# One decoder block: the first weight half goes to the head of SyncE's DMA queue, the norm weights to GpSimd's

## The chip, the core and the metric

The program runs on one core of a Trainium2 chip. The metric is the device time of one execution in microseconds, as the median of several runs; lower is better. The engines are named as in the profile: PE is TensorE's matmul side, PEld its weight load, DVE is VectorE, ACT is ScalarE, POOL is GpSimd, and SP is SyncE, which here only issues DMAs. A "q" behind an engine's name (SPq, ACTq, POOLq) is its queue of instructions that are not counted as busy, DMA issues among them.

## The reference

One layer of a decoder block in fp32, for 512 tokens (S) of width 1024 (D). The part that this change touches is the very beginning:

```python
h = rmsnorm(x, norm_attn_g)
u = h @ w_in                      # q | k | v | u_pool | u_gate
# then: differential attention on q, k, v; a causal pooling of u_pool; sigmoid gates;
x = x + (sigmoid(g_A) * A + sigmoid(g_P) * P) @ w_out
x = x + relu(rmsnorm(x) @ w_up)**2 @ w_down
return rmsnorm(x)
```

## The kernel before

All products are made of three fp32r matmuls: each operand is split into a high part (`hi`, rounded to fp32r) and a low part (`lo`, the rest), and `hi*hi + lo*hi + hi*lo` is summed in PSUM.

The first stage computes V, the values. x arrives transposed, as 8 tiles of 128 x 512 (`xT[k]`, k = 0 to 7), and lands in the tile `gx` (`gt0` in the code). V's weight `w_v` comes in pieces of 128 x 1024 (`wr_v`), each holding the weight rows of two values of k, and each piece is fetched in two halves of 128 x 512, one for each k. In the profile the tile names carry what they hold: `wr_` a raw weight, `wh_` and `wl_` its high and low part, `xh`, `xla` and `xlb` the high and low parts of x times the norm weight (xla for k = 0 to 3, xlb for 4 to 7), `con` the small constants whose first 8 columns are the norm weights `g1c`, `onesr` a 128 x 128 tile of ones.

For each k this has to happen before PE can do its 12 matmuls (three for each of the four token tiles t):

- x's tile lands (L182 issues it on SP's queue; for k = 0 two halves, L143, on ACT's queue);
- ACT multiplies by the norm weight and rounds: `xh` (L184); DVE makes the rest: `xla` or `xlb` (L185). For k = 0 both are done in halves of 256 columns, so that two of the four token tiles can start early. These need `g1c`;
- the weight half lands (L106, L224), ACT casts it (L112, `wh_v`), DVE subtracts (L113, `wl_v`).

PE's three matmuls are L235 (xh by wh), L236 (xh by wl) and L237 (xl by wh). Beside this ACT squares x (L193, L196) and POOL sums the squares into `ssx` (L197). PE also gets matmuls of the first q head as soon as its weight (`wr_q`, split on ACT and DVE as well) is there: L212, L213 and L214, three for each k. All this is issued through a scheduler that orders each engine's instructions from its own model of their times, so a change at the start of the program can reorder instructions further on. Ahead of all this PE is kept busy by 8 matmuls of ones by ones (L170, 16 in the profile), which need nothing but `onesr`.

Of the kernel before, what the change touches and what calls it, by code (L numbers as in the profile page):

```python
# [12 lines left out]
F32R = mybir.dt.float32r  # L13
# [5 lines left out]
P = 128  # L19
# [32 lines left out]
def block_kernel(ctx, tc, xT, x_tok, gains, pos, consts, w_in, w_v, w_pool, w_out, w_up, w_dn, out):  # L52
    nc = tc.nc
    V, A, G, T = nc.vector, nc.scalar, nc.gpsimd, nc.tensor
# [10 lines left out]
    cp = ctx.enter_context(tc.tile_pool(name="cp", bufs=1))  # L65
# [21 lines left out]
    def tmp(tag, name, shape=(P, S), dt=F32, bufs=2):  # L87
        return tp.tile(list(shape), dt, tag=tag, name=name, bufs=bufs)

    def f(ap):  # L90
        return ap.bitcast(F32)
# [4 lines left out]
    def load_w(src, name, nsplit=1, parts=None):  # L96

        nraw[0] += 1
        third = nraw[0] % 3 == 0 and ctx1_open
        raw = (tp if third else wp).tile([P, 1024], F32, tag="wr3" if third else "wr", name=f"wr_{name}", bufs=1 if third else 2)  # L100
        if nsplit == 1:
            nc.sync.dma_start(out=raw, in_=src)
        else:
            w = 1024 // nsplit
            for i in range(nsplit)[parts or slice(None)]:
                nc.sync.dma_start(out=raw[:, i * w : (i + 1) * w], in_=src[:, i * w : (i + 1) * w])  # L106
        hi = wp.tile([P, 1024], F32R, tag="wh", name=f"wh_{name}", bufs=4)
        lo = wp.tile([P, 1024], F32R, tag="wl", name=f"wl_{name}", bufs=4)
        return raw, hi, lo
# [29 lines left out]
    g1c, g2c, gfc, pscc = (con[:, 8 * i : 8 * i + 8] for i in range(4))  # L139

    gt0 = tmp("g", "gx0", (P, 4, S), bufs=1)
    for i in range(2):
        nc.scalar.dma_start(out=gt0[:, 0, i * 256 : i * 256 + 256], in_=xT[0, :, i * 256 : i * 256 + 256])  # L143
    A.preload_act_table_set(EXPLN)
    nc.sync.dma_start(out=g1c, in_=consts[:, 0:8])
    wv0 = load_w(w_v[0, 0], "v0_0", 2, slice(0, 1))
    invc = con[:, 32:40]
    rcc = con[:, 40:56]
    subc = con[:, 56:57]
# [4 lines left out]

    ident = cp.tile([P, P], F32, name="ident")
    make_identity(nc, ident)
    onesr = cp.tile([P, P], F32R, name="onesr")
    ones = f(onesr)
    G.memset(ones, 1.0)
    eps = cp.tile([P, 1], F32, name="eps")  # L160
    G.memset(eps, EPS)
    mask = cf.tile([P, S], F32, name="mask")
# [2 lines left out]
        out=mask[:, 384:512], in_=mask[:, 384:512], pattern=[[-1, P]],  # L165
# [51 lines left out]
    for n in range(2):  # L217
        accs = [bank((0, 1, 2, 3, 4, 5, 6, 0)[4 * n + t], f"v{n}_{t}") for t in range(NT)]
        for kk in range(4):
# [24 lines left out]
            if n == 0 and 0 < kk < 3:  # L244
                i = kk - 1
# [14 lines left out]
        for t in range(NT):  # L260
# [4 lines left out]
                out=vd[2], in0=av, scalar=rcol[:, t, 0:1], in1=vd[1],  # L265
# [26 lines left out]
        out=r_, in0=posf.rearrange("p (t o) -> p t o", o=1).to_broadcast(sh),  # L292
# [700 lines left out]
```

## Time and profile before

| | |
|---|---|
| three runs | 676.32, 676.32, 677.84 us |
| median | 676.32 us |
| profiled execution: span from first to last instruction | 675.2 us |
| PE busy | 665.3 us, 99% of the span |
| DVE, ACT, POOL busy | 529.1, 462.5, 123.0 us |
| first matmul of V (L235) starts | 5.11 us |
| PE's one wait behind the start of V's first pass ends (L237) | 22.20 us |

The profile gives no other time of the profiled execution than its span; the runs' median stands 1.1 us above it. Times in the text are microseconds from the span's start. In a row of the timeline the first number is the start, the second the time, "x2" says that two instructions are merged into the row, and what stands in brackets is how long the engine had been idle before and what ended that. In a row of waits the numbers are the sum, the count and the longest. In a list of DMA issues the last number is the time from issue to landing.

### The profile page before, as it was taken

To read this page: it belongs to the slowest core of one execution; us is meant where nothing else is said; L and a number is where in the kernel's file an instruction comes from. 1 tells how busy PE (TensorE), PEld (TensorE's weight loads), DVE (VectorE), ACT (ScalarE), POOL (GpSimd) and SP (SyncE) were. 2 spreads that over 40 slices of the span, in tenths; PEclk is the share of its full clock that TensorE was granted. 3 is DMA by queue.
4 is the path that set the end of the run, shared out by engine and by line. 5 is a ranking of instruction groups with operands and counts; after the bars stand their busy time and mean duration, and the time that the engine had idled before them with its cause. 6 is when DMAs were issued, how large, how long until landed. Compare 5 with 4: busy or idle time off the path is not lost.

```text
span 675.2 us, 9995 instructions
## 1 busy us (share of the span) xinstructions
PE 665.3 (99%) x3686; PEld 579.9 (86%) x3686; DVE 529.1 (78%) x879; ACT 462.5 (68%) x741; POOL 123.0 (18%) x137
## 2 busy tenths in 40 slices
PE   9999999999999999999999999999999999999995
PEld 7788888888888888888889988899889998899884
DVE  6955877799979986975478989667994599747995
ACT  8465587978887698883477975367753696356874
POOL 6201110132133212520201020202103021210120
PEclk9999999999999999999999999999999999999999
DMA  8526574435254364574964678676969579493863
GB/s 272 189 71 182 126 152 125 102 94 126 87 139 105 101 171 94 126 193 177 309 194 79 196 172 241 153 179 155 234 190 197 200 156 260 125 213 131 213 125 124
DMA packets 32880, 109.34 MB, mean 162 GB/s; under 512 B 4032, under 2 KB 4928, under 8 KB 32832
## 3 DMA queue, kind: packets, MB, share of 16 engines
q0 software_dynamic: 10656, 38.80, 32.4%
q1 hardware_dynamic: 21744, 69.38, 29.0%
q8 instruction: 29, 0.48, 0.3%
q10 hardware_dynamic: 432, 0.52, 0.2%
q14 instruction: 19, 0.16, 0.1%
HBM read 106.59 MB, written 2.10 MB: 161 GB/s over the span
## 4 chain that ended last, share of the span: by engine, by line
PE 86%; DMA 5%; issue 5%; DVE 1%; ACT 1%; SPq 0%; DVEq 0%; POOLq 0%
PE dm L838 7%; PE dm L840 7%; PE dm L841 7%; PE um L759 7%; PE um L764 7%; PE um L761 7%; DMA wga_uNone<-w_up 5%; PE o L417 2%; PE ga L132 2%; PE ga L131 2%; PE gp L135 2%; PE k L132 2%; PE gp L132 2%; PE gp L131 2%; PE k L131 2%
## 5 line engine op out<-in xcount | busy, mean ns | idle before, releaser
L840 PE MATMUL dm<-wh_dt,z 128*128 128x512 f32 (+1 forms) x128 | 49.5, 387 | 0.0
L841 PE MATMUL dm<-wl_dt,z 128*128 128x512 f32 (+1 forms) x128 | 49.4, 386 | 0.0
L838 PE MATMUL dm<-wh_dt,z 128*128 128x512 f32 (+1 forms) x128 | 49.0, 387 | 0.0
L759 PE MATMUL um<-gss,wh_ut 128*128 128x256 f32 x192 | 48.1, 284 | 0.1
L761 PE MATMUL um<-gss,wh_ut 128*128 128x256 f32 x192 | 48.1, 283 | 0.0
L400 ACT ACTIVATE p<-p,st 128x128 f32<-128x128 f32 (+3 forms) x64 | 35.8, 560 | 14.1 <-DVE st L396 13.8
L112 ACT CAST wh_ut<-wga_uNone 128x1024 fp32r<-128x1024 f32 x24 | 24.9, 1053 | 28.8 <-PE dm L840 19.2
L856 DVE TENSOR_TENSOR x<-x,dm 128x512 f32<-128x512 f32 x48 | 32.8, 687 | 14.1 <-PE dm L841 14.0
L670 POOL DMA_DIRECT2D wga_dNone<-w_dn x16 | 14.2, 887 | 151.8 <-DVE wl_dt L113 151.8
L113 DVE TENSOR_TENSOR wl_ut<-wga_uNone,wh_ut 128x1024 fp32r<-128x1024 f32 x24 | 29.0, 1224 | 12.5 <-ACT wh_ut L112 12.5
L112 ACT CAST wh_ub<-wr_u 128x1024 fp32r<-128x1024 f32 x24 | 25.1, 1051 | 19.0 <-PE um L761 10.1
L670 POOL DMA_DIRECT2D wga_uNone<-w_up x18 | 15.6, 867 | 120.9 <-DVE wl_ut L113 86.9
L840 PE MATMUL dm<-wh_db,z 128*128 128x512 f32 x96 | 37.2, 389 | 0.0
L841 PE MATMUL dm<-wl_db,z 128*128 128x512 f32 x96 | 37.2, 389 | 0.0
L759 PEld LDWEIGHTS um<-gss,wh_ut 128*128 128x128 f32 x192 | 36.8, 192 | 0.3 <-ACT rawz L776 0.3
L761 PEld LDWEIGHTS um<-gss,wh_ut 128*128 128x128 f32 x192 | 36.9, 192 | 0.0
L838 PE MATMUL dm<-wh_db,z 128*128 128x512 f32 x96 | 35.8, 390 | 0.0
L113 DVE TENSOR_TENSOR wl_ub<-wr_u,wh_ub 128x1024 fp32r<-128x1024 f32 x24 | 29.2, 1222 | 7.9 <-ACT wh_ub L112 7.9
L112 ACT CAST wh_dt<-wga_dNone 128x1024 fp32r<-128x1024 f32 x24 | 24.8, 1050 | 14.6 <-issue 4.1
L735 DVE TENSOR_TENSOR z<-rawz,z 128x1024 fp32r<-128x1024 f32 x28 | 33.7, 1225 | 0.9 <-ACT z L732 0.9
L396 DVE CUSTOM_DVE_ANT_0 p<-s,mask 128x128 f32<-128x128 f32 (+3 forms) x64 | 30.3, 485 | 3.4 <-PE s L395 3.3
L732 ACT CAST z<-rawz 128x1024 fp32r<-128x1024 f32 x28 | 28.7, 1048 | 6.0 <-DVE rawz L741 4.9
(324 smaller groups left out, 2222.9 us busy)
## 6 DMA issues: line engine op xcount, KB each, us to landing
wr_u<-w_up SPq DMA_DIRECT2D x24, 512.0 KB, 5.3
wr_d<-w_dn SPq DMA_DIRECT2D x24, 512.0 KB, 4.2
wga_uNone<-w_up POOLq DMA_DIRECT2D x18, 512.0 KB, 6.7
wga_dNone<-w_dn POOLq DMA_DIRECT2D x16, 512.0 KB, 5.8
wr_k<-w_in SPq DMA_DIRECT2D x8, 512.0 KB, 3.3
wr_ga<-w_in SPq DMA_DIRECT2D x8, 512.0 KB, 3.3
wr_gp<-w_in SPq DMA_DIRECT2D x8, 512.0 KB, 4.2
wl_ga<-w_in POOLq DMA_DIRECT2D x8, 512.0 KB, 5.5
```

Of the source, the lines that this page charges most:

```text
L112: ins = A.copy(out=hi[:, sl], in_=raw[:, sl])
L113: (eng or G).tensor_tensor(out=lo[:, sl], in0=raw[:, sl], in1=f(hi)[:, sl], op=ALU.subtract)
L131: T.matmul(acc, lhsT=hi[:, c], rhs=rh[:, k, :], start=k == 0, stop=False)
L132: T.matmul(acc, lhsT=hi[:, c], rhs=rl[k], start=False, stop=False)
L400: A.activation(out=pr[:, c, :N], in_=pr[:, c, :N], func=AF.Exp, scale=-1.0, bias=st[:, c : c + 1], accum_out=st[:, 2 + c : 3 + c])
L735: V.tensor_tensor(out=z[:, 1], in0=r, in1=f(z[:, 0]), op=ALU.subtract)
L759: m = T.matmul(a_, lhsT=hi[:, c], rhs=rh[:, k, :], start=p + k == 0 and onto is None, stop=False, skip_group_check=True)
L761: T.matmul(a_, lhsT=hi[:, c], rhs=rl[:, k, :], start=False, stop=False, skip_group_check=True)
L764: m = T.matmul(a_, lhsT=lo[:, c], rhs=rh[:, k, :], start=False, stop=k == 3, skip_group_check=True)
L838: m = T.matmul(a_, lhsT=zh, rhs=hi[:, sl], start=p == 0 and start, stop=False, skip_group_check=True)
L840: T.matmul(a_, lhsT=zl, rhs=hi[:, sl], start=False, stop=False, skip_group_check=True)
L841: end = T.matmul(a_, lhsT=zh, rhs=lo[:, sl], start=False, stop=p == 3, skip_group_check=True)
```

## The change

Four edits, all ahead of the loops:

- `onesr` is set by VectorE (`V.memset`) as its first instruction, and no longer by GpSimd behind the identity's memset;
- the first half of V's first weight is the first DMA on SP's queue, where `g1c` stood;
- `g1c` is fetched by GpSimd's queue, as POOL's first instruction;
- the second half of x's first tile moves from ACT's queue to SP's, behind that weight half.

```diff
     gt0 = tmp("g", "gx0", (P, 4, S), bufs=1)
-    for i in range(2):
-        nc.scalar.dma_start(out=gt0[:, 0, i * 256 : i * 256 + 256], in_=xT[0, :, i * 256 : i * 256 + 256])
+    onesr = cp.tile([P, P], F32R, name="onesr")
+    ones = f(onesr)
+    V.memset(ones, 1.0)
+    nc.scalar.dma_start(out=gt0[:, 0, 0:256], in_=xT[0, :, 0:256])
+    wv0 = load_w(w_v[0, 0], "v0_0", 2, slice(0, 1))
+    G.dma_start(out=g1c, in_=consts[:, 0:8])
     A.preload_act_table_set(EXPLN)
-    nc.sync.dma_start(out=g1c, in_=consts[:, 0:8])
-    wv0 = load_w(w_v[0, 0], "v0_0", 2, slice(0, 1))
+    nc.sync.dma_start(out=gt0[:, 0, 256:512], in_=xT[0, :, 256:512])
...
-    onesr = cp.tile([P, P], F32R, name="onesr")
-    ones = f(onesr)
-    G.memset(ones, 1.0)
```

What this does to the engines' orders shows at three places. The numbers in the names only tell tiles apart (`wr_v0_0` is V's first weight piece, `wr_v0_1` the second; `gx0` is x's tile). First SP's queue at the program's start, before:

```order
L145 DMA con_73<-consts 128x8
L106 DMA wr_v0_0_79<-w_v 128x512
L224 DMA wr_v0_0_79<-w_v 128x512
L182 DMA gx0_74<-xT 128x512 x2
L106 DMA wr_v0_1_163<-w_v 128x512 x2
```

and now:

```order
L106 DMA wr_v0_0_78<-w_v 128x512
L149 DMA gx0_74<-xT 128x256
L224 DMA wr_v0_0_78<-w_v 128x512
L182 DMA gx0_74<-xT 128x512 x2
L106 DMA wr_v0_1_163<-w_v 128x512 x2
```

The weight half is one place earlier, x's second half stands in the place that it left, and everything from L224 on keeps its place.

Second, ACT at the program's start, before:

```order
L143 DMA gx0_74<-xT 128x256 x2
L144 ACT_TABLE_LOAD
L184 ACTIVATE xh_84<-gx0_74,con_73 128x256
L112 CAST wh_v0_0_81<-wr_v0_0_79 128x512
L184 ACTIVATE xh_84<-gx0_74,con_73 128x256
L193 ACTIVATE ssx_110<-gx0_74 128x512
L112 CAST wh_v0_0_81<-wr_v0_0_79 128x512
L184 ACTIVATE xh_84<-gx0_74,con_73 128x512
```

and now:

```order
L145 DMA gx0_74<-xT 128x256
L148 ACT_TABLE_LOAD
L112 CAST wh_v0_0_80<-wr_v0_0_78 128x512
L184 ACTIVATE xh_86<-gx0_74,con_73 128x256 x2
L193 ACTIVATE ssx_110<-gx0_74 128x512
L112 CAST wh_v0_0_80<-wr_v0_0_78 128x512
L184 ACTIVATE xh_86<-gx0_74,con_73 128x512
```

ACT now casts the weight half ahead of both halves of x's first tile.

Third, PE ahead of and in the matmuls for k = 4 (weight piece `v0_2`), and behind those for k = 6 (weight piece `v0_3`), as a difference:

```order
 L213 MATMUL q_115<-xla,wh_q_208 128x512
 L214 MATMUL q_115<-xh,wl_q_209 128x512
-L212 MATMUL q_115<-xh,wh_q_208 128x512
 L235 MATMUL v_0_116<-wh_v_2_218,xh 128x512
 L235 MATMUL v_1_117<-wh_v_2_218,xh 128x512
 L235 MATMUL v_2_118<-wh_v_2_218,xh 128x512
 L235 MATMUL v_3_119<-wh_v_2_218,xh 128x512
-L213 MATMUL q_115<-xla,wh_q_208 128x512
 L236 MATMUL v_0_116<-wl_v_2_219,xh 128x512
```

```order
 L236 MATMUL v_3_119<-wl_v_3_272,xh 128x512
 L237 MATMUL v_3_119<-wh_v_3_271,xlb 128x512
+L212 MATMUL q_115<-xh,wh_q_208 128x512
+L213 MATMUL q_115<-xla,wh_q_208 128x512
 L214 MATMUL q_115<-xh,wl_q_209 128x512
 L235 MATMUL v_0_116<-wh_v_3_271,xh 128x512
```

Two matmuls of the q head have moved from the stretch ahead of k = 5 to behind k = 6. Beside these, PE's first 12 matmuls are in another order (two L236 follow the first two L235 at once), DVE's list begins with the memset and the weight's subtraction, ACT does one square (L196 of k = 6) ahead of a cast instead of behind it, and POOL makes the identity's second step (masks.py:199) later. From V's second pass on the orders are the same.

## The prediction

> **What bounds the kernel now.** I read the page's busy times first, then PE's waits over the whole span, then the chain of work that ended last, and then the first 23 us engine by engine.
>
> ```profile
> PE 665.3 (99%) x3686; PEld 579.9 (86%) x3686; DVE 529.1 (78%) x879; ACT 462.5 (68%) x741; POOL 123.0 (18%) x137
> ...
> PE h2T L629 <- ACT h2f L646: 0.6, 1, 0.6
> PE v L237 <- DVE con L282: 0.3, 1, 0.3
> PE v L235 <- ACT wh_v L112: 0.2, 1, 0.2
> ```
>
> PE is busy for 665.3 of 675.2 us, so at most 10 us can be won without taking matmuls away. The change touches the start, where PE waits twice: 0.2 us for the first cast weight and 0.3 us at an L237. The chain of work says what the second hangs on:
>
> ```profile
> 2.12 4.71 DMA gx<-xT
> ...
> 6.85 0.73 ACT xh L184
> ...
> 20.37 1.77 DVE xlb L185
> 22.15 0.07 DVE con L282
> 22.22 0.48 PE v L237
> ```
>
> The chain goes through SP's fourth DMA (x's tile 1, issued at 2.12, landed at 6.83), then ACT, then DVE up to 22.15 and only there reaches PE. So V's start at 5.11 is not on the path: whatever PE wins at the head it must give back at that L237 unless DVE's low part of x (xlb for k = 5) is ready earlier too. This is the point on which the forecast turns.
>
> **The first weight half.** ACT at the start, and the DMAs that it waits for:
>
> ```profile
> 1.67 1.28 ACT L144 ACT_TABLE_LOAD   x1 [1.67 <-PEq L983]
> 4.44 0.62 ACT L112 CAST wh_v<-wr_v 128x512 fp32r<-128x512 f32 x1 [0.83 <-DMA wr_v<-w_v]
> 4.96 0.51 ACT L184 ACTIVATE xh<-gx,con 128x256 fp32r<-128x256 f32 x1
> 5.37 0.62 ACT L193 ACTIVATE ssx<-gx 128x512 f32<-128x512 f32 x1
> 5.94 0.62 ACT L112 CAST wh_v<-wr_v 128x512 fp32r<-128x512 f32 x1
> 6.85 0.73 ACT L184 ACTIVATE xh<-gx,con 128x512 fp32r<-128x512 f32 x1 [0.29 <-DMA gx<-xT]
> ...
> 0.74 0.38 SPq L145 DMA_DIRECT2D con<-consts  x1
> 1.18 0.42 SPq L106 DMA_DIRECT2D wr_v<-w_v  x1
> ...
> gx<-xT ACTq DMA_DIRECT2D x1, 128.0 KB, 2.3
> wr_v<-w_v SPq DMA_DIRECT2D x1, 256.0 KB, 3.2
> con<-consts SPq DMA_DIRECT2D x1, 4.0 KB, 2.0
> ```
>
> The cast waited 0.83 us for the weight, which was issued at 1.18 and took 3.2 us. At the queue's head it is issued at 0.74. Its time to landing is bounded from below by x's half, 2.3 us for half the bytes, and from above by its own 3.2; I take the middle, 2.75, since it now shares the engines with one half of x instead of two. It lands at 3.5 (3.05 to 3.95). The table load has ended by then (one DMA issue less on ACT's queue, 0.45 us by the distance of two issues on SP; nobody waits for it). The cast then runs from 3.5 to 4.1, and ACT's next instruction starts 0.52 us after it (4.44 to 4.96), at 4.02.
>
> **The norm weights by POOL.** They are now needed at 4.02, before at 3.1. No such small DMA on POOL's queue is in the trace; the nearest rows are POOL's first big one and the small one on SP's queue, each with the stretch in which its first packets appear:
>
> ```profile
> wl_u<-w_in POOLq DMA_DIRECT2D x1, 512.0 KB, 5.6
> q0 software_dynamic: 11, 0.05, 264.0%
> DMA packets 6, 0.00 MB, mean 0 GB/s; under 512 B 6, under 2 KB 6, under 8 KB 6
> L122 POOL DMA_DIRECT2D wl_u<-w_in x1: 999/999/999, 60.5 to 60.5; - x1
> ```
>
> POOL's DMA, issued at 60.5, has no packet on its queue q0 in the stretch 60.4 to 62.2 and its first 11 in 62.2 to 62.4 (second line): 1.7 us. On SP's queue the first 6 packets of the program fall before 1.75 (third line), 1.0 us after the issue at 0.74. So POOL costs 0.7 us more: 2.0 + 0.7 = 2.7 us to landing as the lower bound, and 5.6 us, with 128 times the bytes, as the upper. The small row is far nearer in size; with 0.3 us for standing beside 384 KB of weight and x, I take 3.0: landed at 3.75, hidden behind the cast by 0.3 us. At the upper bound it lands at 6.35. ACT's order past that point (0.41 each for the two halves of xh, 0.57 for the square, 0.62 for the second cast, by the distances of starts above) leaves xh for k = 1 at its old 6.85 if the first half starts by 4.85, so that is how late the constants may be without any cost to the chain.
>
> The Trainium skill, DMA: Bandwidth & Descriptors, Specifications, gives about 1 us to the first byte for GpSimd's path and 0.6 for SyncE's; the trace has 1.7 and 1.0, so the measurement decides. By the page's 0.4 us the constants would land at 3.45 and the sum be the same.
>
> On POOL the issue (1.0 us, last line above) stands ahead of the memsets, where `onesr`'s 0.2 us goes away, so POOL's preparation ends 0.8 us later. The next thing on POOL, the first sum of squares at 8.18, comes after 2.25 us of idling (its row is below). That is the cover; 1.4 us of it is left.
>
> **The warm-up matmuls, and PE's start.**
>
> ```profile
> 0.88 0.20 POOL L159 MEMSET onesr<- 128x128 f32 x1
> ...
> 1.14 0.58 PE L170 MATMUL warm<-onesr 128*128 128x128 f32 x1 [1.14 <-POOL onesr L159]
> 4.07 0.85 PE L170 MATMUL warm<-onesr 128*128 128x128 f32 x3
> 5.11 1.22 PE L235 MATMUL v<-wh_v,xh 128*128 128x512 f32 x2 [0.19 <-ACT wh_v L112]
> 6.13 0.78 PE L235 MATMUL v<-wh_v,xh 128*128 128x512 f32 x2
> 6.75 0.40 PE L236 MATMUL v<-wl_v,xh 128*128 128x512 f32 x1
> ```
>
> DVE has nothing before 3.6, so its memset can start with the program, at about 0.70, and take about POOL's 0.20: PE starts at 0.95 instead of 1.14, and the warm-up's last matmul ends at 4.73 instead of 4.92 (4.07 + 0.85). The first xh half ends at 4.02 + 0.51 = 4.53, so V starts at 4.6, as the next matmul's start overlaps the last one's end (by about 0.2: 0.40 us each, 0.23 apart, below). These first matmuls run slowly: 1.02 us for the first two (5.11 to 6.13), 0.62 for the next two, of which the second already has the later pace of 0.23, so about 0.4 for a slow one. By 6.5 half a microsecond of earlier start has bought only one matmul (starts at 4.6, 5.1, 5.6, 6.0 and 6.4 against 5.1, 5.6, 6.1 and 6.5): PE's lead at k = 1 is 0.23 to 0.33; I take 0.28. The subtraction that L236 needs, DVE's first real work, ends at 4.1 + 0.69 and is wanted at 5.6.
>
> **The two moved matmuls, and the sum.** Further on:
>
> ```profile
> 17.43 0.39 PE L212 MATMUL q<-xh,wh_q 128*128 128x512 f32 x1
> 18.34 1.07 PE L235 MATMUL v<-wh_v,xh 128*128 128x512 f32 x4
> 21.51 0.39 PE L236 MATMUL v<-wl_v,xh 128*128 128x512 f32 x1
> 22.20 0.50 PE L237 MATMUL v<-wh_v,xlb 128*128 128x512 f32 x1 [0.30 <-DVE con L282]
> ...
> 8.74 1.32 DVE L185 SCALAR_TENSOR_TENSOR xla<-gx,con,xh 128x512 fp32r<-128x512 f32 x1 [0.39 <-ACT xh L184]
> 13.40 0.74 DVE L185 SCALAR_TENSOR_TENSOR xla<-gx,con,xh 128x512 fp32r<-128x512 f32 x1
> 20.37 1.77 DVE L185 SCALAR_TENSOR_TENSOR xlb<-gx,con,xh 128x512 fp32r<-128x512 f32 x1
> ...
> 8.18 1.33 POOL L197 TENSOR_TENSOR ssx<-ssx,sq 128x512 f32<-128x512 f32 x1 [2.25 <-ACT sq L196]
> 18.61 2.99 POOL L197 TENSOR_TENSOR ssx<-ssx,sq 128x512 f32<-128x512 f32 x2 [1.01 <-ACT sq L196]
> ...
> GB/s 0 0 0 13 212 332 324 279 283 254 258 303 328 385 393 373 381 414 402 406 406 389 397 389 385 377 184 8 0 160 328 365 213 322 287 269 246 319 244 294
> ```
>
> PE's pace is 0.227 us a matmul (four from 17.43 to 18.34). In the old order it would reach that L237 at 21.74 and waits until 22.20, 0.46 us by starts. In the new one L212 and L213 are no longer ahead of it: PE is there at 21.74 - 0.28 - 0.45 = 21.0. But xlb for k = 5 comes when DVE has made it, and the two matmuls are still to be done afterwards: **+0.45 us** behind the wait.
>
> DVE's end is the other term. From 8.74 to 22.14 DVE does not pause, and its order there is unchanged. One such operation takes 0.74 us where no sum of squares runs on POOL and 1.77 where one does; seven sums fall into this stretch, from 8.18 to 21.6. The chain starts with x's tile 1, which stays fourth on SP's queue with the same 768 KB of x and weight ahead of it. It can gain only from DMA engines idle at the start: of the 40 slices of the first 20 us (last line) the fifth has 212 GB/s and the sixth 332, which is 60 KB or 0.18 us. So the chain moves by 0 to -0.18; I take -0.1.
>
> Sum: -0.1 + 0.45 = **+0.35 us**: 675.2 becomes 675.55, and with the 1.1 us between span and median 676.32 becomes 676.7. That is no change: 0.3%, 2.0 us, is about what a measurement can tell here, and three runs of before spread over 1.5 us. PE's wait at the L237 should grow to about 1.1 us, and the start of V, half a microsecond earlier, be lost in it.
>
> **The rivals.** *DVE's chain gets shorter (faster).* ACT now makes the square for k = 6 ahead of a cast, so the sums shift against DVE's work; if one falls behind xlb for k = 5, the chain is 1.03 us shorter (1.77 - 0.74). Then DVE ends at 21.1, PE is there at 21.0: -1.1 + 0.45 = -0.7, 675.6. For it: the sums lie as close as 18.61 and 20.1 to the chain's end. Against: the shift makes them earlier, and the squares set them before the end in either order.
>
> PE's pace before 6.5 bears on this price. The Trainium skill, TensorE: Matmul & The Clock Gate, Part 1, says that the clock opens after one busy window of 3.4 us that does not start with the program; the trace, with the switch 5.3 us after the first warm-up matmul, agrees. By that rule the switch could as well come 6.8 us after it, at 7.75: PE's lead would be -0.3 instead of 0.28 and this rival 676.2; the forecast stays as it is, since PE would still wait for DVE.
>
> *The constants come late (slower).* Each microsecond beyond 4.85 is one on ACT's xh for k = 1 and so on DVE's chain. At 5.5 the sum is +0.45 + 0.65 = +1.1, 677.4; at the upper bound, 6.35, +1.95, 678.3. It decides against the kernel (over 2.0 us) from a landing at 6.4 on, 5.7 us after the issue. For it: the only POOL row has 5.6 us. Against: that one moves 512 KB, its first packets come after 1.7 us.
>
> [...]
>
> *The change does nothing for the weight:* it shares the DMA engines with x and lands at 3.95 or later. V starts at 5.1; PE still waits for DVE, and the sum is +0.45, 676.8.
>
> **How the numbers follow.** Forecast 0.60, the weight no earlier 0.14 (the same time within a measurement's reach), DVE's chain shorter 0.12, constants late 0.14, of which 0.04 beyond the bound. With 0.02 on each side for a median drawn by the runs' spread: faster 0.03, same 0.91, slower 0.06. The range goes from the shorter chain, less 0.1 (675.5), to the constants at 5.5 plus 0.5 of the runs' spread (677.9). The likeliest case alone is 676.3 to 677.2.
>
> **What would show it.** V's first L235 at 4.5 to 4.7; its cast at 3.5 with no later wait for `con`; the warm-up from 0.95; L212 and L213 for k = 2 behind k = 6; a wait of about 1.1 us at the L237; xlb for k = 5 ending at 22.0 to 22.15, and PE 0.35 us later from there to the end. Wrong would be: xh's first half held by `con` beyond 4.85, DVE's chain ending a microsecond off, or a wait that is new anywhere behind 30 us.

## The result, and the profile after

The changed kernel takes 678.31 us (median of 21 runs, 676.84 to 680.1), the kernel before 676.8 beside it (21 runs, 676.02 to 678.71): a ratio of 1.002, 95% interval 1.0014 to 1.0027, so 1.4 us slower. The forecast was 676.7, in a range that ended at 677.9. The profiled execution has a span of 676.5 us against 675.2.

PE's waits in the profile of the changed kernel (microseconds in total, times, longest):

```profile
PE v L236 <- DVE wl_v L113: 1.2, 2, 0.9
PE warm L170 <- DVE onesr L144: 1.1, 1, 1.1
PE h2T L629 <- ACT h2f L646: 0.9, 1, 0.9
PE v L235 <- ACT xh L184: 0.8, 1, 0.8
PE um L759 <- ACT gss L602: 0.2, 1, 0.2
```

The 0.2 and 0.3 us of before have become 0.8 us ahead of V and 1.2 us behind DVE. The timeline of the same execution (start, duration, engine, line) shows what came late:

```profile
0.74 0.38 SPq L106 DMA_DIRECT2D wr_v<-w_v  x1
1.26 0.72 POOL L147 DMA_DIRECT2D con<-consts  x1 [0.82 <-POOLq L983]
4.24 0.62 ACT L112 CAST wh_v<-wr_v 128x512 fp32r<-128x512 f32 x1 [1.78 <-DMA wr_v<-w_v]
4.76 0.91 ACT L184 ACTIVATE xh<-gx,con 128x256 fp32r<-128x256 f32 x2
6.90 0.62 ACT L112 CAST wh_v<-wr_v 128x512 fp32r<-128x512 f32 x1 [0.70 <-DMA wr_v<-w_v]
7.55 0.72 ACT L184 ACTIVATE xh<-gx,con 128x512 fp32r<-128x512 f32 x1
```

Its DMA rows (the last number is the median time from issue to landing), and the step of its chain that goes through x's tile 1:

```profile
wr_v<-w_v SPq DMA_DIRECT2D x1, 256.0 KB, 3.5
...
con<-consts POOLq DMA_DIRECT2D x1, 4.0 KB, 3.5
```

```profile
2.12 5.41 DMA gx<-xT
```

The weight half, issued 0.44 us earlier, took 3.5 us instead of 3.2 and was cast at 4.24 instead of 4.44. The norm weights were issued at 1.26, not at 0.74, and landed at 4.74. The second weight half held its cast until 6.90 (5.94 before), and x's tile 1, issued at 2.12 as before, took 5.41 us instead of 4.71. Each DMA has 16 completions in the trace: of those of x's tile 1 the ninth came at 5.9 (6.1 in before) and the last at 7.52 (6.82). So not the stream is late, but a few of its parts; of the weight half's too twelve were in by 3.67 and the last at 4.22. The timeline of PE and DVE behind that:

```profile
1.06 3.44 PE L170 MATMUL warm<-onesr 128*128 128x128 f32 x16 [1.06 <-DVE onesr L144]
5.33 0.74 PE L235 MATMUL v<-wh_v,xh 128*128 128x512 f32 x2 [0.82 <-ACT xh L184]
18.59 1.07 PE L235 MATMUL v<-wh_v,xh 128*128 128x512 f32 x4
20.59 0.50 PE L236 MATMUL v<-wl_v,xh 128*128 128x512 f32 x1 [0.94 <-DVE wl_v L113]
34.88 1.02 PE L251 MATMUL pr<-ssx,onesr 128*128 128x512 f32 x2
...
17.05 1.78 DVE L185 SCALAR_TENSOR_TENSOR xlb<-gx,con,xh 128x512 fp32r<-128x512 f32 x1
18.76 3.47 DVE L113 TENSOR_TENSOR wl_v<-wr_v,wh_v 128x512 fp32r<-128x512 f32 x2
22.15 1.40 DVE L185 SCALAR_TENSOR_TENSOR xlb<-gx,con,xh 128x512 fp32r<-128x512 f32 x2
```

PE's wait itself is for DVE's `wl_v` for k = 4, which ends at 20.55; from 20.59 on PE runs without a pause and reaches the first L237 of k = 5 at 22.99, 0.1 us after xlb for k = 5. The two splits thus bind PE at nearly the same point, and the end of that xlb serves below as the mark of DVE's chain.

These rows give the sum of this one execution. DVE's xlb for k = 5 ends at 22.89 (the first half of the last row: 22.15 + 0.74) instead of 22.14, 0.75 us later, which is the 0.70 of x's tile 1. And PE starts the next product (L251) at 34.88 instead of 33.67: 1.21 us, of which 0.75 is DVE's chain and 0.46 stands behind it, the two moved matmuls (52 matmuls from the end of that xlb to L251, 50 in before). The span ends 1.28 us later.

A further 0.25 us lies outside the span. Time less span is 1.80 to 1.96 us in every run of before in the groups below and 2.05 to 2.41 in the changed kernel's. From 676 to 680 us, about and behind the span's end, the DMA view of the changed kernel has one queue at work, with one packet:

```profile
q14 instruction: 1, 0.01, 0.6%
```

One more block of instructions is fetched there. Before has no such packet. Of the 20 traces of this study (the changed kernel has two) the packet is in all 15 whose runs have a median time less span of 1.96 to 2.32, and in none of the five where it is 1.85 to 1.89. Moving the program's end alone wasn't tried, so this is an association, though one without an exception.

### The profile page after: what moved, and what is told of

Its sections match the earlier page's. It is cut to its first block, busy times and chain, and to the rows that moved or that the text cites. A ratio compares the mean times of both kernels' runs of the same rounds, so it can differ in the third digit from the quotient of the medians.

```text
span 676.5 us, 9995 instructions
## 1 busy us (share of the span) xinstructions
PE 665.2 (98%) x3686; PEld 578.9 (86%) x3686; DVE 529.8 (78%) x880; ACT 461.6 (68%) x741; POOL 122.7 (18%) x137
## 4 chain that ended last, share of the span: by engine, by line
PE 87%; DMA 5%; issue 4%; ACT 2%; DVE 1%; SPq 0%; DVEq 0%; POOLq 0%
PE dm L838 7%; PE dm L840 7%; PE dm L841 7%; PE um L759 7%; PE um L764 7%; PE um L761 7%; DMA wga_uNone<-w_up 4%; PE o L417 2%; PE ga L132 2%; PE ga L131 2%; PE gp L135 2%; PE k L132 2%; PE gp L132 2%; PE gp L131 2%; PE k L131 2%
## 5 line engine op out<-in xcount | busy, mean ns | idle before, releaser
L112 ACT CAST wh_ub<-wr_u 128x1024 fp32r<-128x1024 f32 x24 | 25.1, 1048 | 20.0 <-PE um L761 10.7
L670 POOL DMA_DIRECT2D wga_uNone<-w_up x18 | 15.6, 864 | 121.3 <-DVE wl_ut L113 108.9
L113 DVE TENSOR_TENSOR wl_dt<-wga_dNone,wh_dt 128x1024 fp32r<-128x1024 f32 x24 | 29.1, 1220 | 4.5 <-ACT wh_dt L112 4.5
```

The costliest lines, as they stand in the source:

```text
L112: ins = A.copy(out=hi[:, sl], in_=raw[:, sl])
L113: (eng or G).tensor_tensor(out=lo[:, sl], in0=raw[:, sl], in1=f(hi)[:, sl], op=ALU.subtract)
```

## The experiments

Before was run with each group of kernels, and the ratios are to it. "Span" is the difference of the median span to before's in the same group (for the first row of the changed kernel, where no spans of before were kept, to 674.9, the median of its 141 later ones); the last three columns are from the one profiled execution, "clock" being the start of its granted-clock record at full speed.

| kernel | ratio, 95% interval | span, us | x tile 1 landed | V's first L235 | clock |
|---|---|---|---|---|---|
| before | | | 6.82 | 5.11 | 6.4 |
| changed | 1.002 [1.0014, 1.0027] | +1.3 | 7.52 | 5.33 | 4.0 |
| after_again | 1.0014 [1.0005, 1.0023] | +0.8 | 7.2 | 6.05 | 9.9 |
| con_sp2 | 1.0028 [1.0017, 1.004] | +1.85 | 8.1 | 4.99 | 4.8 |
| con_sp2_spare | 1.0029 [1.0019, 1.004] | +2.1 | 8.4 | 5.01 | 4.0 |
| before_late2 | 1.0003 [0.9994, 1.0012] | +0.1 | 6.5 | 5.20 | 4.3 |
| con_act0 | 1.0016 [1.0008, 1.0025] | +0.9 | 6.4 | 5.31 | 4.1 |
| x_sp | 1.0036 [1.0024, 1.0048] | +1.9 | 8.4 | 4.68 | 5.3 |
| wfirst | 1.0009 [1.0001, 1.0018] | +0.6 | 5.8 | 5.11 | 4.9 |
| x_act | 1.002 [1.0012, 1.0029] | +1.1 | 6.1 | 6.12 | 5.1 |
| sp_4k | 1.0011 [1.0002, 1.0019] | +0.75 | 7.9 | 4.86 | 5.8 |
| sp_128k | 1.0014 [1.0006, 1.0022] | +0.9 | 7.6 | 4.99 | 5.2 |
| only_ones | 1.0001 [0.999, 1.0013] | -0.2 | 6.7 | 5.43 | 5.4 |
| con_act0_xact | 1.0026 [1.0014, 1.0038] | +1.85 | 6.4 | 6.50 | 4.0, shut 7.4 to 10.8 |
| after_act_extra | 1.0019 [1.001, 1.0028] | +0.95 | 7.1 | 5.77 | 9.8 |
| after_nosum | 1.0006 [0.9991, 1.0021] | -0.3 | 7.3 | 6.20 | 9.7 |
| before_nosum | 0.9994 [0.9985, 1.0003] | -0.55 | 6.7 | 4.86 | 4.5 |
| after_q0 | 1.0017 [1.0008, 1.0026] | +1.05 | 6.6 | 5.55 | 10.2 |
| after_nosum_warm | 0.9993 [0.9984, 1.0002] | -0.2 | 6.0 | 5.29 | 4.1 |
| after_warm | 1.0021 [1.0011, 1.0031] | +1.6 | 6.6 | 5.21 | 4.0 |

### GpSimd's DMA, and the moved matmuls

My first theory was that GpSimd's DMA holds some of the DMA engines back, and with them the large transfers around it. after_again is the changed kernel unedited.

> The changed kernel once more, unedited: does its profile repeat? In its first profile two of the 16 DMA engines finish V's first weight half 0.6 us behind the others and stay behind (second half landed at 6.87 instead of 5.92 before, x's tile 1 at 7.52 instead of 6.82). If that belongs to the kernel: tile 1 again between 7.3 and 7.7, the low part of x for k = 5 ready at 22.7 to 23.0, and 1.2 to 1.5 us slower than before. If it was chance of one execution: tile 1 at 6.6 to 6.9 and 0.4 to 0.6 us slower.

The slowdown is there again, but in another place: V's first matmul came at 6.05, PE ran the next ones at half pace, and no wait for DVE followed. ACT and PE of that execution:

```profile
5.49 0.91 ACT L184 ACTIVATE xh<-gx,con 128x256 fp32r<-128x256 f32 x2 [1.00 <-DMA con<-consts]
...
6.05 1.22 PE L235 MATMUL v<-wh_v,xh 128*128 128x512 f32 x2 [1.21 <-ACT xh L184]
7.93 0.63 PE L235 MATMUL v<-wh_v,xh 128*128 128x512 f32 x1
8.35 0.63 PE L236 MATMUL v<-wl_v,xh 128*128 128x512 f32 x1
```

ACT waited 1.00 us for the norm weights (landed at 5.47), and PE's starts are 0.42 us apart, where the changed kernel's first profile has 0.23 at the same place.

```
# con_sp2: the changed kernel with
-    G.dma_start(out=g1c, in_=consts[:, 0:8])
+    nc.sync.dma_start(out=g1c, in_=consts[:, 0:8])
# con_sp2_spare: con_sp2, and besides
+    G.dma_start(out=spare, in_=consts[:, 0:8])
# before_late2: before, L212 and L213 for k = 2 held behind the last L237 of k = 6
```

> The changed kernel with the norm weights as SyncE's second DMA instead of GpSimd's first; PE's and ACT's orders are those of the changed kernel. Theory P (GpSimd's DMA itself holds two DMA engines back): V's second weight half lands by 6.1, x's tile 1 by 6.9, and the time is 0.5 to 0.9 us below the changed kernel's, so 0.45 to 0.9 above before. Theory R (one queue now feeds nearly all the first transfers, or the weight at its head does it): tile 1 lands at 7.3 or later and the time stays 1.2 to 1.5 us above before.

> As the kernel with the norm weights on SyncE's queue, but GpSimd also fetches the same 4 KB into a tile that nobody reads, as its first instruction. Theory P: the two late DMA engines are back, tile 1 lands at 7.3 to 7.7, 1.2 to 1.5 us above before, although nobody waits for this DMA. Theory L (the norm weights' own lateness costs): no different from the kernel without it, 0.4 to 0.9 above before.

> The kernel before with one edit in the order alone: the matmuls L212 and L213 for k = 2 are held behind k = 6, as in the changed kernel. Theory O: PE waits 0.45 us longer at the L237 for k = 5 (0.9 us between starts instead of 0.46 over the pace), and ends 0.45 us later, 0.07% slower. Rival: PE catches up later, no change to the start of the second pass (35.3 us).

The theory fell. Without any DMA on GpSimd's queue the kernel is slower still, and one that fetches 4 KB there for nobody changes the span by 0.25 us, within the spread. con_sp2 mends V's start (4.99) and ruins x's tile 1 (8.1).

before_late2 shows the order term in PE's wait. In the time it doesn't stand out: the interval, 0.9994 to 1.0012, holds both nothing and 0.47 us.

```profile
PE v L237 <- DVE xlb L185: 0.8, 1, 0.8
```

That was 0.3 in before. From the end of xlb for k = 5 to the start of L251 PE needs 11.52 us in before (22.15 to 33.67) and as much in sp_4k and sp_128k, which keep its order; it is 12.0 in before_late2 and 11.99, 11.99 and 11.96 in the changed kernel, con_sp2 and con_sp2_spare: 0.47 us.

### Which queue, which place

```
# con_act0: the norm weights first on ScalarE's queue, else as changed
# x_sp: before, x's second half on SyncE's queue behind the first weight half
# wfirst: before, SyncE's first two DMAs exchanged
# x_act: changed, x's second half back on ScalarE's queue
```

> The changed kernel with the norm weights taken from GpSimd's queue and issued first on ScalarE's queue, ahead of x's first half; the weight half stays first on SyncE's queue and x's second half stays second there. SyncE's order of DMAs is that of the changed kernel, word for word. Small-piece theory (the norm weights' 128 pieces of 32 B stall the DMA engines when they come among large pieces, not when they come first): the norm weights land at 2.6 to 3.0 us, weight half b by 6.1 and x tile 1 by 6.9, as before the change (5.92 and 6.82 or 5.44 and 6.46 in two executions); time 676.6 to 677.4. Queue theory (with x's second half on SyncE's queue, the early stream goes through one queue and is slower): weight half b lands at 6.4 or later, x tile 1 at 7.2 or later, time 677.9 to 679. Weight-first theory (two large transfers that start at once spread the engines apart): late as well, 6.4 and 7.2 or more, 677.9 to 679.

> The kernel before with one thing changed: x's second half moves from ScalarE's queue to SyncE's queue behind the weight half, as in the changed kernel. The norm weights stay first on SyncE's queue, ones stays with GpSimd. Queue theory: weight half b lands at 6.4 or later and x tile 1 at 7.2 or later, time 677.9 to 679. Small-piece theory and weight-first theory: weight half b 5.5 to 6.1 plus at most the one issue of 0.47 us that now stands ahead of it, x tile 1 6.5 to 7.0 plus the same at most; time 676.7 to 677.6.

> The kernel before with one thing changed: on SyncE's queue the weight half goes ahead of the norm weights, which are second. x's halves both stay on ScalarE's queue, ones stays with GpSimd. Queue theory: no delay, weight half b by 6.1, x tile 1 by 6.9, time 676.5 to 677.3. Small-piece theory: the norm weights come among large pieces, weight half b at 6.4 or later, x tile 1 at 7.2 or later, time 677.9 to 679.2, as the changed kernel with the norm weights second on SyncE's queue (7.03 and 8.11; 679.2). Weight-first theory: the same lateness as the small-piece theory.

> The changed kernel with x's second half back on ScalarE's queue; the weight half stays first on SyncE's queue, the norm weights on GpSimd's queue and ones with VectorE. Queue theory: weight half b lands by 6.1 and x tile 1 by 6.9, time 676.6 to 677.4. Small-piece theory: the norm weights still land among large pieces, weight half b at 6.4 or later, x tile 1 at 7.2 or later, time 677.8 to 679. Weight-first theory: as late as by the small-piece theory.

x_sp carries the verdict: before with x's second half on SyncE's queue alone is 1.9 us slower in its span. The stretch from 3.5 to 6.5 us (busy time and instructions of PE, PEld, DVE, ACT and POOL, the granted clock, the DMA engines' share and GB/s), first x_sp, then before:

```profile
3.50:6.50 3.00, 3.00 (x14) 2.63 (x14) 1.60 (x3) 1.66 (x4) 1.91 (x5) 1.00 0.69 181
```

```profile
3.50:6.50 3.00, 2.81 (x10) 2.29 (x10) 1.61 (x3) 2.17 (x5) 2.34 (x5) 1.00 1.00 284
```

In this execution, with one transfer of 128 KB moved from one queue to the other, all of them together moved 100 GB/s less; con_sp2 has 216 there. SyncE also issues x's tile 1 later with it, at 2.58 instead of 2.12. (0.23 us of x_sp's span are PE's order, in which one step of the first product has moved as well: 11.75 us from xlb's end to L251.) The changed kernel itself, whose queue holds no norm weights, has 295: it loses time at a few late completions, not in the rate. The small-piece theory, as the whole cause, falls with wfirst, where the norm weights come among large transfers and x's tile 1 lands at 5.8, and with x_sp, where they come first and it lands at 8.4. The weight-first theory falls with the same two.

The queue theory is not whole either. con_act0 was to be as late as the changed kernel. Its median span is late (+0.9 us), while its profile, the second shortest of its 11 executions, has x's tile 1 on time. x_act brought x's tile 1 forward to 6.1, as it was to, and is no faster than the changed kernel, because the norm weights, which GpSimd's queue landed at 5.54, held ACT (its rows, and PE's wait):

```profile
5.56 0.51 ACT L184 ACTIVATE xh<-gx,con 128x256 fp32r<-128x256 f32 x1 [1.03 <-DMA con<-consts]
...
7.42 0.71 ACT L184 ACTIVATE xh<-gx,con 128x512 fp32r<-128x512 f32 x1
...
PE v L237 <- DVE con L282: 0.7, 1, 0.7
```

From 5.56 on ACT has no pause, so it gets to xh for k = 1 only at 7.42, 1.3 us after that tile has landed (6.85 and 0.03 us in before). xlb for k = 5 ends 15.30 us behind it, at 22.72, as it does 15.30 us behind it in before, and PE waits for it. The clock has no part in this execution: its record begins at 5.14.

```
# sp_4k: before, and behind the first weight half
+    nc.sync.dma_start(out=rb[:, 0:8], in_=consts[:, 0:8])
# sp_128k: before, and at the same place
+    nc.sync.dma_start(out=rb[:, 0:256], in_=xT[0, :, 256:512])
# only_ones: before, ones set by VectorE
# con_act0_xact: con_act0, x's second half on ScalarE's queue too
```

> The kernel before with one DMA more on SyncE's queue, third, between the two weight halves: 4 KB of the norm weights once more (128 pieces of 32 B), into a tile that nothing reads before it is written anew. TensorE's order is word for word that of before. Slot theory (every DMA ahead on SyncE's queue costs what stands behind it a place, whatever its size): x tile 1 lands 0.6 to 0.9 us later than in before (from 6.5 to 6.8 to 7.3 to 7.7), the span grows by 0.7 to 1.3 us. Bytes theory (what counts is how many bytes stand ahead): 4 KB are nothing, span and time within 0.3 us of before. Issue theory (SyncE's issuing of 0.47 us is passed on): 0.3 to 0.5 us.

> The same as the 4 KB one, with 128 KB in 128 pieces of 1 KB (x's second half once more) as the additional third DMA on SyncE's queue. Slot theory: the same cost as the 4 KB one within 0.3 us, span plus 0.7 to 1.3 us. Bytes theory: 128 KB at the 230 to 390 GB/s of this stretch are 0.33 to 0.57 us, span plus 0.3 to 0.6, and that much more than the 4 KB one. Issue theory: plus 0.3 to 0.5, as the 4 KB one.

> The kernel before with one change alone: ones is set by VectorE, ahead of everything else there; all DMAs and TensorE's order are those of before. By every theory the early DMAs land as before and TensorE's first matmul comes 0.05 to 0.1 us earlier (1.06 for 1.14): span within 0.3 us of before. If the 0.24 us more that the changed kernel takes outside its span comes with this step, the time is 0.2 to 0.3 us longer with the span unchanged.

> The norm weights first on ScalarE's queue and both of x's halves behind them there; SyncE's queue begins with the weight's two halves and x tile 1, with neither the norm weights nor an x half ahead; ones with VectorE. Slot theory: two DMAs fewer ahead of x tile 1 than the changed kernel's queue with the norm weights second, one fewer than before's: x tile 1 lands at 5.2 to 6.1 us (before 6.5 to 6.8), the first matmul of V at 4.7 to 5.3, span 0.5 to 1.0 us shorter than before: time 675.6 to 676.3. Bytes theory: the same bytes in the same stretch, x tile 1 at 6.2 to 6.8, time 676.3 to 677.1. Weight-first theory (two large transfers at once spread the engines): x tile 1 at 7.2 or later, time 677.5 to 678.5.

4 KB and 128 KB at the same place cost about the same, 0.75 and 0.9 us of span. So the bytes theory does not fit the medians, though the 0.3 us that it allowed for 4 KB is still within that run's interval: a DMA more ahead on SyncE's queue costs about that, whatever it carries. Its own issue, 0.47 us, is within both intervals, so I can't say that the place costs more than the issuing. Against x_sp, sp_128k differs in that x's second half is also fetched on ScalarE's queue, and used from there, and in the 0.23 us of PE's order; with 128 KB more to move it is the faster of the two (1.0014 against 1.0036, intervals that just don't meet).

The Trainium skill, DMA: Bandwidth & Descriptors, Issuing engines are not separate DMA queues, says that transfers of all issuing engines run on the same 16 DMA engines and that starting them from several engines saves only the time to initiate them. The profile of x_sp does not agree with it (181 and 284 GB/s above, one execution each).

con_act0_xact missed in another way: with three DMAs on ScalarE's queue, x's first half, the second of them, landed only at 5.6 and V began at 6.50. Its windows, in the same columns:

```profile
4.00:6.50 2.50, 0.48 (x4) 0.29 (x3) 1.12 (x2) 1.18 (x4) 1.21 (x4) 1.00 0.92 340
6.50:7.30 0.80, 0.80 (x3) 0.67 (x4) 0.80 (x3) 0.80 (x2) 0.00 (x0) 1.00 1.05 405
7.40:10.70 3.30, 3.30 (x10) 2.53 (x9) 2.48 (x4) 3.30 (x8) 1.64 (x2) 0.50 1.05 389
10.80:14.10 3.30, 3.30 (x16) 2.71 (x15) 3.30 (x4) 3.30 (x7) 1.90 (x2) 1.00 0.74 269
```

PE idles for 2.0 us ahead of 6.50, and from 7.4 to 10.7 its clock is granted at 0.50, with 10 matmuls where the next stretch has 16. This is what after_again had shown as pace alone: there the record begins only at 9.9.

only_ones, whose change touches nothing but the warm-up's start, had by chance the prediction's other rival in its profile. DVE's operations around xlb for k = 5:

```profile
17.93 1.28 DVE L113 TENSOR_TENSOR wl_v<-wr_v,wh_v 128x512 fp32r<-128x512 f32 x2
19.13 1.78 DVE L185 SCALAR_TENSOR_TENSOR xlb<-gx,con,xh 128x512 fp32r<-128x512 f32 x1
20.90 1.72 DVE L185 SCALAR_TENSOR_TENSOR xlb<-gx,con,xh 128x512 fp32r<-128x512 f32 x1
```

One collision with a sum of squares fell behind k = 5, the chain ended at 20.91 instead of 22.14, and the span was 674.1. The 12 runs' median is that of before.

### The chain or the clock

```
# after_act_extra: changed, and x's second half once more
+    nc.scalar.dma_start(out=rb[:, 0:256], in_=xT[0, :, 256:512])
# after_nosum, before_nosum: six of the seven sums left out
-            G.tensor_tensor(out=ssx, in0=ssx, in1=sq, op=ALU.add)
+            None if k < 7 else G.tensor_tensor(out=ssx, in0=ssx, in1=sq, op=ALU.add)
# after_q0: changed, the first product's steps up to k = 2 ahead of V's k = 4
```

> The changed kernel with one DMA more on ScalarE's queue, its second: x's second half once more (128 KB), into a tile that nothing reads before it is written anew; the half that is used still comes through SyncE's queue. TensorE's order is that of the changed kernel. Empty-queue theory (the early stream is slow because ScalarE's queue has run dry and one queue alone is served more slowly): weight half b lands by 6.4 and x tile 1 by 7.2 although 128 KB more are read, span 0.3 to 1.0 us below the changed kernel's 676.1. Bytes theory: 128 KB more to read, 0.3 to 0.6 us above it. Third possibility (what counts is the place in SyncE's queue alone): within 0.2 us of it.

> The changed kernel without six of GpSimd's seven sums of squares (L197, k = 1 to 6), so the row norms of x are not the reference's; everything else, and TensorE's, VectorE's, ScalarE's and SyncE's order, is as in the changed kernel. It takes away what slows VectorE's splits, and leaves the DMAs and TensorE alone. Chain theory (the lateness reaches the end through VectorE's chain of splits that starts with x tile 1): VectorE gets ahead, TensorE no longer waits for it, span 1.0 to 2.0 us below the changed kernel's 676.1. TensorE theory (the lateness is that of V's first matmul and of the clock after it): within 0.3 us of the changed kernel.

> The kernel before without the same six sums of squares, so its row norms are not the reference's. Chain theory: TensorE's lead over VectorE in before is small, so what there is to gain is 0.3 to 1.0 us; and the changed kernel without the sums is then 0.0 to 0.6 us behind this one where with them it is 1.2 us of span behind. TensorE theory: within 0.3 us of before, and the distance between the two stays at 1.2 us of span.

> The changed kernel with the first product's step k = 2 put ahead of V's k = 4, the step that the change had moved behind k = 6; the DMAs are those of the changed kernel. Order theory: its two matmuls fill 0.45 us of TensorE's wait for the last split, span 0.3 to 0.6 us below the changed kernel's 676.1, time 677.5 to 677.9 with before at 676.9. Rival (the wait for the last split is set by VectorE alone and the moved matmuls are done in other waits): within 0.2 us of the changed kernel.

The spans of after_act_extra and after_q0 (675.9 and 676.0) stay within 0.3 us of the changed kernel's (676.2 and 676.0). In both profiled executions the clock opened at about 10, so that PE was behind DVE, and neither an earlier x tile nor a better order could show.

The sums tell more. Without them the splits that slow down beside them take 0.74 instead of 1.77 us, DVE is far ahead in both kernels, and the median distance shrinks from 0.8 to 1.3 us of span to 0.25. But the median hides something, for the means are still 0.9 us apart. Without the sums before's spans lie together (673.5 to 675.2), while the changed kernel's spread out: 673.3 to 674.4 six times, as before's, and 674.9 to 678.3 six times, five of them above all of before's. The profiled one, 676.2, is of this upper half; its start:

```profile
6.20 1.22 PE L235 MATMUL v<-wh_v,xh 128*128 128x512 f32 x2 [1.36 <-ACT xh L184]
7.22 1.05 PE L236 MATMUL v<-wl_v,xh 128*128 128x512 f32 x2
8.07 0.63 PE L235 MATMUL v<-wh_v,xh 128*128 128x512 f32 x1
```

Half pace after an idle time of 1.36 us, and the clock's record begins at 9.71. The last two runs fill that idle time:

```
-    for _ in range(8):
+    for _ in range(11):
         T.matmul(warm[:, :P], lhsT=ones, rhs=ones, start=True, stop=True)
```

> The changed kernel without six of GpSimd's seven sums of squares (its row norms of x are not the reference's), and with eleven instead of eight warm-up products, so that TensorE is busy until about 6.1 us at half pace instead of 4.84, when V's first matmul becomes ready. The run without the longer warm-up had spans in two groups, 673.3 to 674.4 and 674.9 to 678.3, six each. Clock theory (the upper group are executions in which TensorE's idle time of 0.7 to 1.4 us ahead of V puts the opening of its clock off by one window of 3.4 us, to 9.7 to 10.2): the idle time is gone, the clock opens by 7.9 in every execution, the upper group goes: all spans between 673.5 and 675.7, median 674.2 to 674.9. Other-cause theory (the upper group comes from late transfers): it stays, some three or more of eleven spans above 675.7.

> The changed kernel, complete, with eleven instead of eight warm-up products and nothing else. Both-limits theory (two lateness paths stand side by side, TensorE's by V's late start and the clock, and VectorE's by x tile 1's landing; each alone gives a start of the next product at about 35): with the clock mended VectorE's chain still ends 27.0 to 27.4 us after x tile 1's landing, so span and time stay within 0.5 us of the changed kernel's 676.1 and 678.1, with before at 676.9. Clock-alone theory: the longer warm-up brings the span down by 0.8 us or more, to 675.3 or less. Chain-alone theory: no change, within 0.2 us.

Without the sums no span is above before's range any more, where five of twelve were: twelve spans from 673.8 to 675.2. It is another group of runs, and in one execution of each kernel alone the clock is seen (9.71 and 4.13).

```profile
1.06 4.17 PE L170 MATMUL warm<-onesr 128*128 128x128 f32 x22 [1.06 <-DVE onesr L144]
5.29 0.74 PE L235 MATMUL v<-wh_v,xh 128*128 128x512 f32 x2
```

So the clock is one carrier of the lateness, and it is the idle time ahead of V that puts its opening off. after_warm, with the sums in place, is not faster than the changed kernel, as the theory of two limits had it, but it is a poor witness of the size: the scheduler, told of a longer warm-up, moved three more matmuls of the first product behind the wait (12.67 us from xlb's end to L251 instead of 11.99), so its +1.6 holds 0.68 us that the edit did not mean. Its clock opened at 4.02, V began 0.03 us behind the warm-up, and PE still waited 1.6 us for `wl_v`: there DVE's chain is the limit by itself. Leaving the sums out takes 1.8 us of span from this kernel (676.5 to 674.7) and 0.55 from before. So DVE's chain is the other carrier.

None of these kernels beats before. only_ones equals it, and before_nosum, which is not the whole computation, shows that even a free DVE chain would win only 0.55 us of span there.

## Why the prediction was wrong, step by step

**The weight half, 3.5 us (3.05 to 3.95).** It landed at 4.22 in the profile, outside the range, and at 3.9 in after_again. Going first shortened little: over seven executions its time to landing was 3.0 to 3.5 us, not 2.75. In the changed kernel's first profile this step alone moved V: the cast began at 4.24 and xh 0.52 us behind it, when the norm weights were just in (4.74). That the warm-up began at 1.06 and not at 0.95, since DVE's memset came only at 0.84, changed nothing.

**The norm weights, 3.75 us.** This step failed in every profile of that start. The issue began at 1.26, after 0.82 us of idling that GpSimd's own queue ended, and landing took 3.4 to 4.4 us, where I had taken 3.0 between 2.7 and 5.6. In seven profiles with x's second half on SyncE's queue and this DMA on GpSimd's they landed at 4.6 to 5.6.

**"Free until 4.85."** This failed with it, and matters more. I priced late constants only by what they do to ACT's xh for k = 1, that is, to DVE's chain. (By the 0.52 us between the starts of a cast and what follows it, which I used elsewhere, the bound is 4.95.) They also hold V's first matmul, and PE's idle time ahead of it puts the clock's opening off: I had put this at nothing. In four of the five profiles of the changed kernel's start with eight warm-up products ACT waited 0.57 to 1.00 us for the norm weights and the opening came at 9.7 to 10.2 us; in the fifth, the first one, it came at 4.0, ahead of the idle time. With the late opening PE itself is the limit: L251 starts at 34.94 to 35.17 (after_q0, after_again, after_act_extra, after_nosum) without any wait for DVE. V started at 5.3 to 6.2, not at 4.6.

The Trainium skill, TensorE: Matmul & The Clock Gate, Part 1, gives free-running windows of 3413 ns, one busy one of which opens the clock. The trace agrees: con_act0_xact's changes at 7.37 and 10.78 are 3.41 apart. I had worked out a late opening at 7.75, 6.8 us behind the first warm-up matmul, and dropped it "since PE would still wait for DVE". In those four profiles it came 8.7 to 9.1 us behind it, and PE did not wait for DVE at all. The figure of the Trainium skill for how far the moment varies, 500 ns either way in the same section, is too small here: even in the other 16 profiles the record begins between 4.0 and 6.4.

**DVE's chain, -0.1 us.** The mechanism held: from the landing of x's tile 1 to the end of xlb for k = 5 it is 15.33 us in before and 15.37 in the changed kernel, and 15.3 to 15.6 in eleven of the other profiles. The size of its start did not. With the changed kernel's DMAs x's tile 1 landed at 6.0 to 7.5 in seven executions, with before's at 6.5 to 6.8 in four. So this is the term of the sum that was mis-sized: +0.75 where I had -0.1. The step "the same 768 KB ahead of it" counted bytes; by x_sp and sp_4k the queue, and a DMA's place or issue in it, count as well.

**The moved matmuls, +0.45.** Measured 0.47 by the traces, where DVE is the limit. The wait that was to grow to about 1.1 us did so (0.94 us of idling, 1.1 by the distance of starts), but at an L236, for `wl_v`. Where the clock is the limit the order costs nothing: after_q0, which has its two matmuls early, starts L251 at 35.05 all the same.

**The level.** I put 1.1 us between span and median; it is 1.85 to 1.88 for before as the median of each group of runs, and 2.12 in the changed kernel. The first three runs of before had happened to lie below its later median (676.32, later 676.6 to 677.1). That is 0.5 us of the miss.

For the profiled execution the sum thus reads +0.75 and +0.46 instead of -0.1 and +0.45, and +0.25 outside. In the four profiles with the late clock PE's pace stands in place of the first two terms, at about the same price: L251 starts 1.3 to 1.5 us later than in before. How many of the other executions are of either kind is not known. Of the rivals, "the constants come late" came true: in the changed kernel by a path that I had not written, PE's clock, and in x_act by the written one, where constants at 5.54 put xh for k = 1 off by 0.57 us against before, with 0.69 forecast. Why a few completions of a DMA come up to 2.2 us after the median one in the first 8 us stays open: it happened in most kernels with a DMA more on SyncE's queue or with x's second half there, but not in con_act0's profile, and no run here looks at one DMA engine.

## What to carry to other kernels

A late operand at the start is to be priced on every engine that waits for it: in the changed kernel the late constants cost at most 0.2 us on DVE's chain, since x's tile 1 was late too, and a whole clock window on PE, which then was the limit; in x_act, with an earlier tile, they cost the chain 1.3 us. Mending one of two limits that lie within half a microsecond shows nothing in the time, so an experiment that removes one for good (the sums) is needed before the other can be seen. And a transfer that is moved takes a place in a queue, which cost here about as much for 4 KB as for 128.

## What the runs showed that I had not expected

- Taking windows of 3.41 us back and forth from an opening, PE's clock opened in spite of an idle time of up to 0.58 us in its window (only_ones) and did not with 0.71 (after_q0); once open it stood 0.98 us of idling in one window (x_act) and shut after 2.02 (con_act0_xact).
- At the program's start a queue with the norm weights, x's second half and the weight together moves 181 to 229 GB/s from 3.5 to 6.5 us (x_sp, con_sp2, con_sp2_spare), where the other kernels have 271 to 367.
- An instruction block fetched at the program's end goes with 0.1 to 0.45 us of time outside the span.
